# Contrast adjustment of 48 images: three bands on a 192 KB ring in pieces, instead of six tiles in three slots

## The chip, the cores and the metric

The kernel runs on one core of one Trainium2 chip; the seven other cores do nothing. The metric is the device time of one execution in microseconds. The kernel before has a median of 239.43 us over three runs (239.42 to 239.44).

## The reference

```python
# x: (16, 3, 512, 512) float32, factor = 1.5
mean = np.mean(x, axis=(2, 3), keepdims=True)
out = np.clip(mean + factor * (x - mean), 0, 1).astype(np.float32)
```

There are 48 images of 262,144 float32 pixels, 1 MB each. Each needs its own mean before its first output pixel can be computed: out = clip(1.5 x - 0.5 mean). All of x is 50.33 MB, read once, and the output is as large, written once, so 100.66 MB pass between the memory and the core's on-chip buffer. The buffer that the kernel uses for pixels is 192 KB on each of 128 partitions, 25.2 MB, half of x.

## The kernel before, in words

An image lies on 16 partitions with 64 KB (16,384 elements) on each, so a tile of 128 partitions is eight images, 8.39 MB, and x is six tiles, which are contiguous in memory. `ring` has three slots of 64 KB per partition; tile t lives in slot t mod 3 from its load to its store, and is overwritten in place.

All transfers are issued by SyncE (SP) on one DMA queue, in the order of the program: `load` (L77) and `store` (L80). The order is written by hand under `tc.manual_schedule()`: loads of tiles 0, 1, 2, then computation and stores of tiles 0, 1, 2, then loads 3, 4, 5, then computation and stores 3, 4, 5. The semaphore waits are put in from the data's dependences. An instruction that SP holds for a wait holds everything behind it in SP's program; a transfer that is issued goes behind those that were issued earlier.

For each tile `compute` does the following. The sum over a partition's row is split: VectorE reduces the first 4,352 columns (L85, into `sums`), ScalarE passes the other 12,032 through a copy in place with an accumulator (L89). TensorE multiplies each column of sums by `blockw`, a 128x128 matrix that holds (1 - factor)/262144 where two partitions belong to the same image (L100); the products accumulate in the column of `bias` in PSUM that belongs to the tile. Then VectorE computes factor * x + bias (L103) and max 0, min 1 (L106), both in place, and the store is issued. Tile 0 alone is cut: it is loaded in pieces of 8, 24 and 32 KB per partition, summed in two halves, and clipped and stored in pieces of 8 and 56 KB.

Each of the 16 DMA engines moves eight of the 128 rows of a DMA, one packet a row, and then one 4-byte packet that tells the semaphore.

Of the kernel before, what the change touches and what calls it, by code (L numbers as in the profile page):

```python
# [1 line left out]

# [4 lines left out]


P = 128  # L10
ROW = 16384
HALF = ROW // 2
BUFS = 3
SHORT = 2048
SUM = 4352


@with_exitstack
def kernel(
    ctx: ExitStack,  # L20
    tc: tile.TileContext,
    x: bass.AP,
    factor: float,
    out: bass.AP,
):

    nc = tc.nc
    f32 = mybir.dt.float32  # L30
    Alu = mybir.AluOpType
    Act = mybir.ActivationFunctionType

    B, C, H, W = x.shape
    n_img, n_pix = B * C, H * W
    ppi = n_pix // ROW
    per_tile = P // ppi
    n_tiles = n_img // per_tile
    assert ppi * ROW == n_pix and per_tile * n_tiles == n_img

    factor = float(factor)
    wconst = (1.0 - factor) / float(n_pix)

    x_f = x.rearrange("b c h w -> (b c h w)")
    out_f = out.rearrange("b c h w -> (b c h w)")

    def dram(ap, t, c0=0, c1=ROW):
        return bass.AP(tensor=ap.tensor, offset=t * P * ROW + c0, ap=[[ROW, P], [1, c1 - c0]])

    consts = ctx.enter_context(tc.tile_pool(name="consts", bufs=1))  # L50
    xpool = ctx.enter_context(tc.tile_pool(name="xpool", bufs=1))
    small = ctx.enter_context(tc.tile_pool(name="small", bufs=1))
    psum = ctx.enter_context(tc.tile_pool(name="psum", bufs=1, space=bass.MemoryType.PSUM))


    sums = small.tile([P, 4 * n_tiles], f32, name="sums")
    bias = psum.tile([P, n_tiles], f32, name="bias")

    blockw = consts.tile([P, P], f32, name="blockw")
    blocks = blockw.rearrange("p (a b) -> p a b", b=ppi)  # L60
    nc.gpsimd.memset(blockw, wconst)  # L61
    for base, step in ((0, -ppi), (ppi - 1, ppi)):
        nc.gpsimd.affine_select(  # L63
            out=blocks,
            in_=blocks,
            compare_op=Alu.is_ge,
            fill=0.0,
            base=base,
            pattern=[[step, per_tile], [0, ppi]],
            channel_multiplier=1 if step < 0 else -1,  # L70
        )


    ring = xpool.tile([P, BUFS, ROW], f32, name="ring")

    def load(t, c0=0, c1=ROW):
        nc.sync.dma_start(out=ring[:, t % BUFS, c0:c1], in_=dram(x_f, t, c0, c1))  # L77

    def store(t, c0=0, c1=ROW):
        nc.sync.dma_start(out=dram(out_f, t, c0, c1), in_=ring[:, t % BUFS, c0:c1])  # L80

    def add(t, col, c0, c1, c2):
        xt = ring[:, t % BUFS, :]
        own = sums[:, 4 * t + col : 4 * t + col + 2]
        nc.vector.tensor_reduce(  # L85
            out=own[:, 0:1], in_=xt[:, c0:c1], axis=mybir.AxisListType.X, op=Alu.add
        )
        part = xt[:, c1:c2]
        nc.scalar.activation(out=part, in_=part, func=Act.Copy, accum_out=own[:, 1:2])  # L89
        return [own[:, 1:2], own[:, 0:1]]  # L90

    def compute(t, *cuts):
        xt = ring[:, t % BUFS, :]
        if t == 0:
            parts = add(t, 0, 0, SUM, HALF) + add(t, 2, HALF, HALF + SUM, ROW)
        else:
            parts = add(t, 0, 0, SUM, ROW)
        shift = bias[:, t : t + 1]
        for k, part in enumerate(parts):
            nc.tensor.matmul(shift, blockw, part, start=k == 0, stop=k == len(parts) - 1)  # L100
        for c0, c1 in zip((0, *cuts), (*cuts, ROW)):
            part = xt[:, c0:c1]
            nc.vector.tensor_scalar(  # L103
                out=part, in0=part, scalar1=factor, scalar2=shift, op0=Alu.mult, op1=Alu.add
            )
            nc.vector.tensor_scalar(  # L106
                out=part, in0=part, scalar1=0.0, scalar2=1.0, op0=Alu.max, op1=Alu.min
            )
            store(t, c0, c1)

    with tc.manual_schedule():
        load(0, 0, SHORT)
        load(0, SHORT, HALF)
        load(0, HALF, ROW)
        load(1)
        load(2)
        compute(0, SHORT)
        compute(1)
        compute(2)
        load(3)  # L120
        load(4)
        load(5)
        compute(3)
        compute(4)
        compute(5)


# [1 line left out]
_INS = ['x', 'factor']  # L129
_OUTS = [((16, 3, 512, 512), 'float32')]  # L130

_NUMBERS = {'factor': 1.5}


# [26 lines left out]
```

## Time and profile before

| | |
|---|---|
| median of three runs | 239.43 us |
| span of the profiled execution, first to last instruction | 237.30 us |
| median less span | 2.13 us |
| first DMA packet of x starts | 1.82 us |
| last packets of the last store end | 235.43 to 236.08 us |
| VectorE busy | 137.4 us (58%) |
| ScalarE busy | 59.9 us (25%) |
| TensorE busy | 7.9 us (3%) |
| DMA | 2160 packets, 100.66 MB, 98.7% of 16 engines' span |

The profiled execution is given by its span alone; the 2.13 us between the span and the median lie outside the first and last instruction. Times in the views are in microseconds from the start of the span. A GB/s figure of a stretch counts each packet where it starts.

### The profile page before, as it was taken

The page shows a single profiled execution, that of the slowest core. Times are in us where ns is not written, and L with a number is a line of the kernel's source. Part 1 is how long each engine was busy: PE and PEld are TensorE (multiplying, and loading weights), DVE is VectorE, ACT ScalarE, POOL GpSimd, SP SyncE. Part 2 cuts the span into 40 slices and gives each one's busy share as a digit, 9 for nine tenths or more (in the row PEclk, how much of TensorE's full clock was granted, in tenths as well). Part 3 has the DMA queues.
Part 4 walks back from the last instruction along what each step waited for, and adds up shares of the span by engine and source line. Part 5 has one row for each costly group of instructions (what it writes and reads, how often), then busy time and mean ns, then how long its engine had stood idle before and what let it go on. Part 6 is the DMA issues. An engine that isn't in the chain of part 4 may idle for free.

```text
span 237.3 us, 186 instructions
## 1 busy us (share of the span) xinstructions
PE 7.9 (3%) x28; PEld 6.9 (3%) x28; DVE 137.4 (58%) x21; ACT 59.9 (25%) x15; POOL 1.1 (0%) x7
## 2 busy tenths in 40 slices
PE   0010100010001000000000000100000000000000
PEld 0010100010001000000000000100000000000000
DVE  0071899949998998000000043499989998991000
ACT  2051300980492000000000049319509800000000
POOL 1000000000000000000000000000000000000000
DMA  7999989899799798989899998989899998989894
GB/s 289 418 442 442 530 353 530 353 486 398 331 464 454 341 530 353 530 353 519 365 442 442 398 486 353 530 354 530 353 475 409 431 453 376 508 353 530 353 530 177
DMA packets 2160, 100.66 MB, mean 424 GB/s; under 512 B 240, under 2 KB 240, under 8 KB 240
## 3 DMA queue, kind: packets, MB, share of 16 engines
q1 hardware_dynamic: 2160, 100.66, 98.7%
HBM read 50.33 MB, written 50.33 MB: 424 GB/s over the span
## 4 chain that ended last, share of the span: by engine, by line
DVE 43%; DMA 36%; ACT 9%; PE 2%; SPq 1%; issue 0%; DVEq 0%; ACTq 0%
DMA ring<-in_x_dram 36%; DVE ring L103 18%; DVE ring L106 18%; ACT ring L89 9%; DVE sums L85 6%; PE bias L100 2%; SPq L77 1%; SPq L80 0%; DVEq L103 0%; ACTq L89 0%
## 5 line engine op out<-in xcount | busy, mean ns | idle before, releaser
L89 ACT ACTIVATE ring<-ring 128x12032 f32<-128x12032 f32 (+1 forms) x7 | 58.0, 8280 | 128.2 <-DMA ring<-in_x_dram 128.2
L85 DVE TENSOR_REDUCE sums<-ring 128x1 f32<-128x4352 f32 x7 | 32.8, 4683 | 63.9 <-DMA ring<-in_x_dram 63.9
L103 DVE TENSOR_SCALAR ring<-ring,bias 128x16384 f32<-128x16384 f32 (+2 forms) x7 | 52.8, 7538 | 12.9 <-PE bias L100 12.9
L106 DVE TENSOR_SCALAR ring<-ring 128x16384 f32<-128x16384 f32 (+2 forms) x7 | 52.3, 7476 | 0.2
L100 PE MATMUL bias<-sums,blockw 128*128 128x1 f32 x28 | 7.9, 360 | 189.1 <-ACT ring L89 175.4
L100 PEld LDWEIGHTS bias<-sums,blockw 128*128 128x128 f32 x28 | 6.9, 314 | 190.0 <-ACT ring L89 159.4
L89 ACT ACT_TABLE_LOAD x1 | 1.3, 1283 | 0.8 <-PEq L142 0.8
L89 ACT ACTIVATION_READ_ACCUMULATOR ring<-ring 128x1 f32 x7 | 1.3, 187 | 0.0
L63 POOL TENSOR_SCALAR_AFFINE_SELECT blockw<-blockw 128x128 f32<-128x128 f32 x2 | 0.7, 340 | 0.1
L61 POOL MEMSET blockw<- 128x128 f32 x1 | 0.2, 204 | 0.3 <-POOLq L142 0.3
L142 POOL MEMSET const-bfloat16-1.0<- 128x1 bf16 x1 | 0.1, 102 | 0.0
L142 POOL MEMSET const-uint8-127<- 128x1 uint8 x1 | 0.1, 102 | 0.0
L142 POOL MEMSET const-float32-0.0<- 128x1 f32 x1 | 0.1, 98 | 0.3 <-issue 0.3
L142 POOL MEMSET const-float32-1.0<- 128x1 f32 x1 | 0.1, 98 | 0.0
## 6 DMA issues: line engine op xcount, KB each, us to landing
out_dram<-ring SPq DMA_DIRECT2D x1, 7168.0 KB, 35.9
ring<-in_x_dram SPq DMA_DIRECT2D x1, 4096.0 KB, 20.8
ring<-in_x_dram SPq DMA_DIRECT2D x1, 3072.0 KB, 11.6
ring<-in_x_dram SPq DMA_DIRECT2D x1, 1024.0 KB, 4.7
out_dram<-ring SPq DMA_DIRECT2D x1, 1024.0 KB, 34.3
ring<-in_x_dram SPq DMA_DIRECT2D x5, 57.7
out_dram<-ring SPq DMA_DIRECT2D x5, 27.0
```

What stands on the lines that cost most here:

```text
L61: nc.gpsimd.memset(blockw, wconst)
L63: nc.gpsimd.affine_select(out=blocks, in_=blocks, compare_op=Alu.is_ge, fill=0.0, base=base, pattern=[[step, per_tile], [0, ppi]], channel ...
L77: nc.sync.dma_start(out=ring[:, t % BUFS, c0:c1], in_=dram(x_f, t, c0, c1))
L85: nc.vector.tensor_reduce(out=own[:, 0:1], in_=xt[:, c0:c1], axis=mybir.AxisListType.X, op=Alu.add)
L89: nc.scalar.activation(out=part, in_=part, func=Act.Copy, accum_out=own[:, 1:2])
L100: nc.tensor.matmul(shift, blockw, part, start=k == 0, stop=k == len(parts) - 1)
L103: nc.vector.tensor_scalar(out=part, in0=part, scalar1=factor, scalar2=shift, op0=Alu.mult, op1=Alu.add)
L106: nc.vector.tensor_scalar(out=part, in0=part, scalar1=0.0, scalar2=1.0, op0=Alu.max, op1=Alu.min)
L142: nc = _bacc.Bacc("TRN2", target_bir_lowering=False, num_devices=1)
```

## The change

An image now lies on eight partitions with 128 KB (32,768 elements) on each, so 128 partitions hold a band of sixteen images, and x is three bands of 16.8 MB. The ring is the same 192 KB per partition, now without slots: the column c (0 to 384 KB over the three bands) lives at c mod 192 KB. Loads, sums, clips and stores are written in column pieces, named here in KB per partition; band 0 is 0 to 128, band 1 is 128 to 256, band 2 is 256 to 384. The 15 DMAs become 24: 12 loads and 12 stores, of 8, 24, 32 or 64 KB per partition. In memory the rows of a DMA are now 128 KB apart, before 64 KB. A shared piece is summed by VectorE (44%) and ScalarE (56%), a piece with `shared=False` by ScalarE alone. All transfers stay on SP's one queue.

```diff
-ROW = 16384
-HALF = ROW // 2
-BUFS = 3
-SHORT = 2048
-SUM = 4352
+ROW = 32768
+KB = 256
+RING = 192 * KB
+SHARE = 0.56
...
-    ring = xpool.tile([P, BUFS, ROW], f32, name="ring")
+    ring = xpool.tile([P, RING], f32, name="ring")
+    def piece(c0, c1):
+        first = c0 % RING
...
+        return ring[:, first : first + c1 - c0]
-    def load(t, c0=0, c1=ROW):
-        nc.sync.dma_start(out=ring[:, t % BUFS, c0:c1], in_=dram(x_f, t, c0, c1))
+    def load(*edges):
+        for c0, c1 in zip(edges, edges[1:]):
+            nc.sync.dma_start(out=piece(c0 * KB, c1 * KB), in_=dram(x_f, c0 * KB, c1 * KB))
...
+    def add(*edges, shared=True):
+        for c0, c1 in zip(edges, edges[1:]):
+            band = c0 * KB // ROW
+            shift = bias[:, band : band + 1]
+            begin, end = c0 * KB == band * ROW, c1 * KB == (band + 1) * ROW
+            mid = c0 * KB + (round((c1 - c0) * KB * (1 - SHARE) / 64) * 64 if shared else 0)
+            parts = []
+            if shared:
...
+                nc.vector.tensor_reduce(
+                    out=own, in_=piece(c0 * KB, mid), axis=mybir.AxisListType.X, op=Alu.add
+                )
...
+            part = piece(mid, c1 * KB)
+            nc.scalar.activation(out=part, in_=part, func=Act.Copy, accum_out=own)
...
+                nc.tensor.matmul(
+                    shift, blockw, own, start=begin and k == 0, stop=end and k == len(parts) - 1
+                )
+    def clip(*edges):
...      # per piece: the two tensor_scalar as before, then store(c0, c1)
     with tc.manual_schedule():
-        load(0, 0, SHORT)
-        load(0, SHORT, HALF)
-        load(0, HALF, ROW)
-        load(1)
-        load(2)
-        compute(0, SHORT)
-        compute(1)
-        compute(2)
-        load(3)
-        load(4)
-        load(5)
-        compute(3)
-        compute(4)
-        compute(5)
+        load(0, 8, 32, 64, 96, 128, 160, 192)
+        add(0, 8, shared=False)
+        add(8, 32, 64, 96, 128)
+        add(128, 160, 192, shared=False)
+        clip(0, 8, 32, 64, 96, 128)
+        load(192, 224, 256, 320)
+        add(192, 224, 256)
+        clip(128, 160, 192)
+        add(256, 320, shared=False)
+        load(320, 352, 384)
+        clip(192, 256)
+        add(320, 352, 384)
+        clip(256, 288, 320, 352, 384)
```

More of the change, by code (lines that the diff above doesn't have):

```diff
@@ L36 @@
     ppi = n_pix // ROW
-    per_tile = P // ppi
-    n_tiles = n_img // per_tile
-    assert ppi * ROW == n_pix and per_tile * n_tiles == n_img
+    per_band = P // ppi
+    n_bands = n_img // per_band
+    assert ppi * ROW == n_pix and per_band * n_bands == n_img
     factor = float(factor)
@@ L45, with dram @@
     out_f = out.rearrange("b c h w -> (b c h w)")
-    def dram(ap, t, c0=0, c1=ROW):
-        return bass.AP(tensor=ap.tensor, offset=t * P * ROW + c0, ap=[[ROW, P], [1, c1 - c0]])
+    def dram(ap, c0, c1):
+        band, col = divmod(c0, ROW)
+        return bass.AP(
+            tensor=ap.tensor, offset=band * P * ROW + col, ap=[[ROW, P], [1, c1 - c0]]
+        )
     consts = ctx.enter_context(tc.tile_pool(name="consts", bufs=1))
@@ L53 @@
     psum = ctx.enter_context(tc.tile_pool(name="psum", bufs=1, space=bass.MemoryType.PSUM))
-    sums = small.tile([P, 4 * n_tiles], f32, name="sums")
-    bias = psum.tile([P, n_tiles], f32, name="bias")
+    sums = small.tile([P, 32], f32, name="sums")
+    bias = psum.tile([P, n_bands], f32, name="bias")
     blockw = consts.tile([P, P], f32, name="blockw")
@@ L68 @@
             base=base,
-            pattern=[[step, per_tile], [0, ppi]],
+            pattern=[[step, per_band], [0, ppi]],
             channel_multiplier=1 if step < 0 else -1,
         )
-    ring = xpool.tile([P, BUFS, ROW], f32, name="ring")
-    def load(t, c0=0, c1=ROW):
-        nc.sync.dma_start(out=ring[:, t % BUFS, c0:c1], in_=dram(x_f, t, c0, c1))
[L79 to L104, printed above, removed]
+    ring = xpool.tile([P, RING], f32, name="ring")
@@ new lines, in piece, with store @@
+    def piece(c0, c1):
+        first = c0 % RING
+        assert c0 // ROW == (c1 - 1) // ROW and first + c1 - c0 <= RING
+        return ring[:, first : first + c1 - c0]
+    def load(*edges):
+        for c0, c1 in zip(edges, edges[1:]):
+            nc.sync.dma_start(out=piece(c0 * KB, c1 * KB), in_=dram(x_f, c0 * KB, c1 * KB))
+    def store(c0, c1):
+        nc.sync.dma_start(out=dram(out_f, c0 * KB, c1 * KB), in_=piece(c0 * KB, c1 * KB))
+    used = [0]
+    def add(*edges, shared=True):
[6 more added lines that the diff above has]
+            if shared:
+                own = sums[:, used[0] : used[0] + 1]
+                used[0] += 1
+                nc.vector.tensor_reduce(
+                    out=own, in_=piece(c0 * KB, mid), axis=mybir.AxisListType.X, op=Alu.add
+                )
+                parts.append(own)
+            own = sums[:, used[0] : used[0] + 1]
+            used[0] += 1
+            part = piece(mid, c1 * KB)
+            nc.scalar.activation(out=part, in_=part, func=Act.Copy, accum_out=own)
+            parts.append(own)
+            for k, own in enumerate(parts):
+                nc.tensor.matmul(
+                    shift, blockw, own, start=begin and k == 0, stop=end and k == len(parts) - 1
+                )
@@ L105, in compute @@
+    def clip(*edges):
+        for c0, c1 in zip(edges, edges[1:]):
+            band = c0 * KB // ROW
+            part = piece(c0 * KB, c1 * KB)
+            nc.vector.tensor_scalar(
+                out=part,
+                in0=part,
+                scalar1=factor,
+                scalar2=bias[:, band : band + 1],
+                op0=Alu.mult,
+                op1=Alu.add,
             )
@@ L108, in compute @@
             )
-            store(t, c0, c1)
+            store(c0, c1)
     with tc.manual_schedule():
-        load(0, 0, SHORT)
-        load(0, SHORT, HALF)
-        load(0, HALF, ROW)
-        load(1)
-        load(2)
-        compute(0, SHORT)
-        compute(1)
-        compute(2)
-        load(3)
-        load(4)
-        load(5)
-        compute(3)
-        compute(4)
-        compute(5)
+        load(0, 8, 32, 64, 96, 128, 160, 192)
[11 more added lines that the diff above has]
+        clip(256, 288, 320, 352, 384)
 _INS = ['x', 'factor']
```

## The prediction

> **What bounds the kernel now.** I read the page first, its DMA rows and its queue.
>
> ```profile
> span 237.3 us, 186 instructions
> ...
> PE 7.9 (3%) x28; PEld 6.9 (3%) x28; DVE 137.4 (58%) x21; ACT 59.9 (25%) x15; POOL 1.1 (0%) x7
> ...
> DMA  7999989899799798989899998989899998989894
> ...
> q1 hardware_dynamic: 2160, 100.66, 98.7%
> ...
> DVE 43%; DMA 36%; ACT 9%; PE 2%; SPq 1%; issue 0%; DVEq 0%; ACTq 0%
> ```
>
> The chain gives VectorE 43% and the DMA 36%, yet the one queue's engines are occupied for 98.7% of the span. The packet records decide: put end to end, each engine's 135 packets run from 1.82 us to between 235.43 and 236.08 us without a gap (each starts 3 or 4 ns before its predecessor ends). So no wait of the chain reaches the end time: the queue always had the next transfer. The end is the sum of the packets, plus 1.82 us in front and 1.22 us from the last packet to the end of the span.
>
> Packets have fixed durations by row: 8 KB 0.309 us, 24 KB 0.912, 32 KB 1.213, 56 KB 2.116, 64 KB 2.418, in both directions. The exceptions are in the next view, the windows (length, engines' busy times, granted clock, DMA share, GB/s).
>
> ```profile
> 38.60:57.92 19.32, 1.01 (x4) 0.93 (x4) 16.25 (x3) 10.32 (x2) 0.00 (x0) 1.00 1.00 434
> 57.92:61.36 3.44, 0.00 (x0) 0.00 (x0) 3.44 (x1) 0.00 (x0) 0.00 (x0) 1.00 1.03 305
> ...
> 155.55:174.90 19.35, 1.17 (x4) 1.00 (x4) 18.56 (x4) 10.32 (x2) 0.00 (x0) 1.00 1.00 434
> 174.90:177.46 2.56, 0.00 (x0) 0.00 (x0) 2.56 (x1) 0.00 (x0) 0.00 (x0) 1.00 0.99 410
> ```
>
> Each first window holds eight 64 KB rows per engine, the second the last row of load 2 and of load 5. After each the queue turns from loads to stores. There all sixteen rows took longer than 2.418 us: 3.532 on average at the first turn, 2.55 at the second. A turn from loads to stores cost 1.11 and 0.13 us. The turn back (load 3 after store 2, near 122 us) lengthened one row of one engine by 0.19, a mean of 0.01. Beyond the start-up no other row is long.
>
> **The change, part by part.** The head is the same: the first loads are again 8, 24 and 32 KB. So is the tail from last packet to end.
>
> Row pieces. With the 4 ns overlap a 64 KB row costs 2.4145 us of an engine, two 32 KB rows 2 x 1.2095 = 2.419: a split costs 4.5 ns. Per engine there were 15 DMAs x 8 = 120 rows, now 24 x 8 = 192: 72 x 4.5 ns = 0.32 us. Nine more semaphore packets of 9 ns less overlap: 0.05. Together +0.37 us. A Trainium skill rule speaks against this edit: "DMA: Bandwidth & Descriptors", Anatomy of one DMA, gives each (GpSimd-issued) DMA about 2.0 us of fixed cost; nine more in series would be 18 us, some 257 us in all. The trace disagrees for queued transfers: across its 14 boundaries the next packet follows within nanoseconds.
>
> Turns. Loads turn to stores at load 160-192, load 256-320 and load 352-384: three times, not twice. The first again leads from loads into an 8 KB store, the first store of all, as the 1.11 did; I carry it over. Of the other two one replaces load 5 (0.13). The new one lies between 0.13 and 1.11; by its row sizes (64 KB load, 32 KB store) it is nearest to 0.13, where a 64 KB store followed; for its smaller rows I take 0.30. Nothing excludes that 32 KB rows make turns cheaper; that is a rival. The second turn back is 0.01.
>
> Engines and waits cost nothing if the queue stays fed, so I walked the queue. Prices come from the groups by shape.
>
> ```profile
> L89 ACT ACTIVATE ring<-ring 128x12032 f32<-128x12032 f32 x5 | 51.2, 10231 | 111.2 <-DMA ring<-in_x_dram 111.2
> L103 DVE TENSOR_SCALAR ring<-ring,bias 128x16384 f32<-128x16384 f32 x5 | 43.8, 8757 | 12.3 <-PE bias L100 12.3
> L106 DVE TENSOR_SCALAR ring<-ring 128x16384 f32<-128x16384 f32 x5 | 43.5, 8695 | 0.2
> L85 DVE TENSOR_REDUCE sums<-ring 128x1 f32<-128x4352 f32 x7 | 32.8, 4683 | 63.9 <-DMA ring<-in_x_dram 63.9
> ...
> L89 ACT ACTIVATE ring<-ring 128x3840 f32<-128x3840 f32 x2 | 6.8, 3402 | 17.0 <-DMA ring<-in_x_dram 17.0
> L103 DVE TENSOR_SCALAR ring<-ring,bias 128x2048 f32<-128x2048 f32 x1 | 1.3, 1292 | 0.7 <-PE bias L100 0.7
> L106 DVE TENSOR_SCALAR ring<-ring 128x2048 f32<-128x2048 f32 x1 | 1.2, 1227 | 0.0
> ```
>
> Two shapes of a row give a slope: ScalarE (10.231 - 3.402)/8192 = 0.83 ns a column plus 0.2 us, each clip pass 0.521 plus 0.2. A 32 KB piece (8,192 columns) then takes 2 passes, 4.48 + 4.43 = 8.9 us on VectorE, against 8 x 1.2095 = 9.68 us on the queue: VectorE gains 0.8 us on it with every piece. Its share of a sum (3,584 columns) takes 3.9 us by L85's mean, ScalarE's 4,608 columns 4.0 plus 0.2 to read the accumulator; landing follows the last packet by 0.3, the matmuls take 0.6.
>
> The walk, with 19.3 us for a 64 KB piece on the queue:
> - Load 96-128 lands at 41.6 us; sums and matmul end at 46.6; clips of band 0 end at 49, 56, 65, 74 and 83. The queue is busy with loads to 61.8 (where it was before too), then runs out after each store at 64, 72, 81, 91, 101. Each store is issued over 5 us ahead.
> - SP then holds load 192-224 (wait on stores 0-8 and 8-32, long landed) and 224-256, issued about 84; load 256-320 waits for store 96-128, 101 us, with 19 us of loads queued. Behind it on SP stand stores 128-160 and 160-192, not computed yet.
> - Load 224-256 lands at about 120.3. VectorE has its reduces first, ScalarE ends at 124.6, matmul 125.2, clip 128-160 ends at 134.2, and SP issues at 134.6. The queue has load 256-320 until 139.2. With 0.6 us from issue to packet, 4 us are to spare. This is the tightest place.
> - Load 320-352 waits for store 128-160 (about 149.7) while 160-192 still has 9 us to run; load 352-384 likewise. Store 192-256, behind both on SP, is issued at 161 with the queue full to 178. The 64 KB ScalarE sum 256-320 (13.9 us from 139.5) is done at 153.4; nobody needs it before 178.
> - Load 352-384 lands at 178.6, clip 256-288 ends at 192.5, the queue is busy with store 192-256 to 198: 4.5 us to spare. The last three stores gain 0.8 us each.
>
> So nothing runs dry. Before, store 5 was issued at 214.6 with store 4's last packets landing at 217.1, a margin of 2.5 us less the 0.6, and lost nothing.
>
> The sum: +0.37 + 0.30 + 0.01 = +0.68. The profiled span of 237.30 becomes 237.98; the median stands 2.13 us above it, so 240.11, said as 240.1. The nearest row alone (0.13) gives 239.94, the far end (1.11) 240.92.
>
> **Rivals.**
> - No change that shows (chance 0.16): 32 KB rows make the new turn free, or two turns cheaper; 239.43 + 0.37 = 239.8. A measurement of this kernel can tell about 0.2%, 0.48 us, from no change, which would hide this. For it: the second turn was only 0.13.
> - Faster (0.10): the excess of a turn belongs to the row size. The long rows were 64 KB; now two of three turns end on 32 KB loads, the first included. If the three together cost 0.2 us instead of the 1.24 of before, it is 0.37 - 1.04 = -0.67: 238.8. It decides once the three sum to under 0.39. Against it: both turns of before ended on 64 KB rows and differ eightfold, so the load's row size is not what sets it.
> - The queue runs dry (0.06): store 128-160 is issued too late because band 1's sums end later than I count. It decides from 4 us; every microsecond beyond is lost for good, since the end is the sum of packets and gaps. Sums 6 us late would cost 2: 242.1. For it: VectorE and ScalarE both work on the last piece at once, which L85 and L89 did before too. Against: their instructions repeat to some 10 ns in the trace.
> - The row pitch (0.08): the 128 streams lie 128 KB apart instead of 64. One per cent on 232 us of packets is 2.3 us, so 242.4 with the sum; it decides from 0.2%, a 32 KB row of 1.216 us. Against: rows of 8, 24, 32 and 56 KB on the 64 KB pitch fit one line with the contiguous ones. The Trainium skill ("DMA: Bandwidth & Descriptors", Latency and other measured facts) reports HBM copies slowing with large power-of-two pitches, 207 GB/s at 512 KiB where a padded pitch gave 214, and more beyond; it has no figure for 128, and no run here shows one.
>
> **How the numbers follow.** The forecast has 0.60 as slower by over 0.2%; with pitch and dry queue that is 0.74. Same 0.16, faster 0.10. The range goes from 239.4 (free turns and somewhat less) to 241.6 (the far end of the turn, plus a dry spell or pitch loss of 0.7 us), leaving out most of the faster case and the worse halves of the last two.
>
> **What would show it.** 3,456 packets; 32 KB rows at 1.213 us; the queue at 434 GB/s between turns; long rows only ahead of stores 0-8, 128-160 and 192-256; store 128-160 issued near 134.6; span near 238.0. A gap in the engines' packets near 139 or 198, or 32 KB rows above 1.216 us, makes it wrong on the slow side; a total of turns under 0.39 us on the fast side.

## The result, and the profile after

The changed kernel takes 258.51 us (median of four runs, 258.17 to 259.07) against 239.43 in the same comparison: a ratio of 1.0795, 95% interval 1.0779 to 1.0811. It is 19.1 us slower, where 0.7 us slower was forecast. The profiled execution took 258.63 us and its span is 256.9, 1.7 less. Later executions of the kernel before show the same 1.7 (239.44 us with a span of 237.7), so the profiled execution of before was probably some 0.4 us faster than its median, and only 1.7 of the 2.13 us lie outside the span. That would account for the spans differing by 19.6 us and the medians by 19.1.

The page after, the lines that answer to those shown of before:

```profile
span 256.9 us, 233 instructions
...
PE 10.4 (4%) x40; PEld 9.4 (4%) x40; DVE 136.3 (53%) x32; ACT 63.6 (25%) x25; POOL 1.2 (0%) x7
...
DMA  7999999993037899998999999999999998999996
...
q1 hardware_dynamic: 3456, 100.66, 91.9%
...
DMA 45%; DVE 38%; ACT 6%; SPq 2%; PE 1%; another core or an unknown queue 1%; issue 0%
```

The packet count is the 3,456 that was forecast, and VectorE's busy time hardly differs from before. But the queue's share fell from 98.7% to 91.9%, and the row of slices shows where: "9303" is a hole near 60 to 85 us, and nothing like it follows. The windows of the changed kernel put edges on the hole (columns as before; the last two are DMA share and GB/s):

```profile
0.00:61.00 61.00, 5.20 (x20) 4.72 (x20) 14.61 (x4) 25.99 (x13) 1.22 (x7) 1.00 0.97 413
61.00:72.90 11.90, 0.59 (x2) 0.50 (x2) 3.38 (x3) 7.12 (x2) 0.00 (x0) 1.00 0.00 0
72.90:75.50 2.60, 0.00 (x0) 0.00 (x0) 2.57 (x2) 0.00 (x0) 0.00 (x0) 1.00 0.98 403
75.50:79.80 4.30, 0.00 (x0) 0.00 (x0) 4.30 (x2) 0.00 (x0) 0.00 (x0) 1.00 0.17 74
79.80:87.10 7.30, 0.00 (x0) 0.00 (x0) 7.26 (x2) 0.00 (x0) 0.00 (x0) 1.00 0.91 387
87.10:88.60 1.50, 0.00 (x0) 0.00 (x0) 1.50 (x2) 0.00 (x0) 0.00 (x0) 1.00 0.51 218
88.60:255.76 167.16, 4.64 (x18) 4.21 (x18) 102.73 (x22) 30.49 (x10) 0.00 (x0) 1.00 0.99 425
```

The loads end at 61 us and for 11.9 us nothing moves; then stores 0-8, 8-32 and 32-64 run with smaller holes in front of the second and third. In the packet records the three holes have a mean of 17.84 us per engine. After 88.6 us the queue is fed to the end. What the first store waited for stands in the timeline of the changed kernel (start, length, instruction, and in brackets the idle time before it with its releaser):

```profile
46.22 1.01 PE L111 MATMUL bias<-sums,blockw 128*128 128x1 f32 x4 [8.69 <-DVE sums L101]
...
51.99 7.03 ACT L108 ACTIVATE ring<-ring 128x8192 f32<-128x8192 f32 x1 [5.58 <-DMA ring<-in_x_dram]
...
61.69 7.03 ACT L108 ACTIVATE ring<-ring 128x8192 f32<-128x8192 f32 x1 [2.58 <-DMA ring<-in_x_dram]
...
68.86 0.59 PE L111 MATMUL bias<-sums,blockw 128*128 128x1 f32 x2 [9.11 <-ACT ring L108]
69.49 1.29 DVE L119 TENSOR_SCALAR ring<-ring,bias 128x2048 f32<-128x2048 f32 x1 [23.33 <-PE bias L111]
...
72.07 0.35 SPq L86 DMA_DIRECT2D out_dram<-ring  x1
```

Band 0's last matmuls are over at 47.2 us. The first clip of band 0 starts at 69.49, directly behind the matmuls of pieces 128-160 and 160-192, which belong to band 1. It reads another column of `bias`, and needs nothing of them. In the built program its wait is for the eleventh matmul of the program; band 0 has nine (each is two instructions in the timeline).

### The profile page after: what moved, and what is told of

The parts are those of the page before. It is cut to its first block, busy times and chain, and to the rows that moved or that the text cites. A ratio compares the mean times of both kernels' runs of the same rounds, so it can differ in the third digit from the quotient of the medians.

```text
span 256.9 us, 233 instructions
## 1 busy us (share of the span) xinstructions
PE 10.4 (4%) x40; PEld 9.4 (4%) x40; DVE 136.3 (53%) x32; ACT 63.6 (25%) x25; POOL 1.2 (0%) x7
## 2 busy tenths in 40 slices
DMA packets 3456, 100.66 MB, mean 392 GB/s; under 512 B 384, under 2 KB 384, under 8 KB 384
## 3 DMA queue, kind: packets, MB, share of 16 engines
q1 hardware_dynamic: 3456, 100.66, 91.9%
## 4 chain that ended last, share of the span: by engine, by line
DMA 45%; DVE 38%; ACT 6%; SPq 2%; PE 1%; another core or an unknown queue 1%; issue 0%
DMA ring<-in_x_dram 39%; DVE ring L119 17%; DVE ring L127 17%; DMA out_dram<-ring 7%; ACT ring L108 6%; DVE sums L101 3%; SPq L83 1%; PE bias L111 1%; SPq L86 0%
## 5 line engine op out<-in xcount | busy, mean ns | idle before, releaser
L108 ACT ACTIVATE ring<-ring 128x4608 f32<-128x4608 f32 (+4 forms) x12 | 61.2, 5101 | 137.8 <-DMA ring<-in_x_dram 137.8
L119 DVE TENSOR_SCALAR ring<-ring,bias 128x8192 f32<-128x8192 f32 (+3 forms) x12 | 53.8, 4487 | 37.7 <-PE bias L111 37.7
L101 DVE TENSOR_REDUCE sums<-ring 128x1 f32<-128x3584 f32 (+1 forms) x8 | 30.1, 3768 | 64.1 <-DMA ring<-in_x_dram 64.1
L127 DVE TENSOR_SCALAR ring<-ring 128x8192 f32<-128x8192 f32 (+3 forms) x12 | 53.1, 4427 | 0.4
L111 PE MATMUL bias<-sums,blockw 128*128 128x1 f32 x40 | 10.4, 358 | 192.6 <-DVE sums L101 134.2
L111 PEld LDWEIGHTS bias<-sums,blockw 128*128 128x128 f32 x40 | 9.4, 320 | 193.5 <-DVE sums L101 134.8
L108 ACT ACTIVATION_READ_ACCUMULATOR ring<-ring 128x1 f32 x12 | 2.2, 186 | 0.0
## 6 DMA issues: line engine op xcount, KB each, us to landing
ring<-in_x_dram SPq DMA_DIRECT2D x1, 3072.0 KB, 11.9
```

The source lines that it names most:

```text
L101: nc.vector.tensor_reduce(out=own, in_=piece(c0 * KB, mid), axis=mybir.AxisListType.X, op=Alu.add)
L111: nc.tensor.matmul(shift, blockw, own, start=begin and k == 0, stop=end and k == len(parts) - 1)
L119: nc.vector.tensor_scalar(out=part, in0=part, scalar1=factor, scalar2=bias[:, band : band + 1], op0=Alu.mult, op1=Alu.add,)
L127: nc.vector.tensor_scalar(out=part, in0=part, scalar1=0.0, scalar2=1.0, op0=Alu.max, op1=Alu.min)
```

## The experiments

Theory A: the first clip waits for matmuls of band 1 that are written ahead of it and write the same PSUM tile, and this empties the queue. Rival B: each of the nine more DMAs costs some 2 us, which would give nearly the same total. Rival C: the rows 128 KB apart are slower.

**One bias tile for each band.**

```diff
-    bias = psum.tile([P, n_bands], f32, name="bias")
+    bias = [psum.tile([P, 1], f32, name=f"bias{k}") for k in range(n_bands)]
...  # bias[:, band : band + 1] becomes bias[band][:, 0:1] in add and in clip
```

> The changed kernel with one edit: bias is three PSUM tiles of one column, one for each band, instead of one tile of three columns, so that the first clip no longer waits for the sums of pieces 128-160 and 160-192. Theory A (the first clip's wait on band 1's matmuls emptied the queue): the clip of piece 0-8 starts near 47 us instead of 69.5, the three gaps in the DMA engines' packets (11.9 + 4.3 + 1.4 us on the first engine) vanish, and the time is 240.1 to 241.5 us. Rival B (each of the nine more DMAs costs about 2 us): 258.5 us, unchanged. Rival C (rows 128 KB apart are slower): at most 1 or 2 us below 258.5.

Measured: 239.56 us (median of 11), 1.0006 times the kernel before, interval 0.9995 to 1.0017. Its timeline and the windows over the place of the hole:

```profile
46.14 1.01 PE L111 MATMUL bias<-sums,blockw 128*128 128x1 f32 x4 [8.70 <-DVE sums L101]
47.19 1.29 DVE L119 TENSOR_SCALAR ring<-ring,bias 128x2048 f32<-128x2048 f32 x1 [1.10 <-PE bias L111]
...
51.91 7.03 ACT L108 ACTIVATE ring<-ring 128x8192 f32<-128x8192 f32 x1 [5.58 <-DMA ring<-in_x_dram]
53.11 3.36 DVE L127 TENSOR_SCALAR ring<-ring 128x6144 f32<-128x6144 f32 x1
...
134.53 9.21 SPq L86 DMA_DIRECT2D out_dram<-ring  x2
```

```profile
61.00:72.90 11.90, 0.59 (x2) 0.50 (x2) 11.87 (x3) 7.12 (x2) 0.00 (x0) 1.00 1.02 438
72.90:88.60 15.70, 0.00 (x0) 0.00 (x0) 10.13 (x3) 0.00 (x0) 0.00 (x0) 1.00 1.00 434
```

The clip's idle time fell from 23.33 to 1.10 us and the holes are gone, with all 24 DMAs and the 128 KB spacing kept. This one wait made the whole loss that can be seen in the time; B and C are out. That it came out 0.5 us under the lower end expected is taken up below.

**The same adds, written later.**

```diff
-        add(128, 160, 192, shared=False)
         clip(0, 8, 32, 64, 96, 128)
+        add(128, 160, 192, shared=False)
```

> The changed kernel with one line moved: add(128, 160, 192, shared=False) behind clip(0, 8, 32, 64, 96, 128), with the single bias tile kept. Theory A: the same cure as separate bias tiles, since what the clip waits for is what was written down before it: 240.1 to 241.5 us, within 0.3 us of the kernel with three bias tiles. Rival A2 (it is VectorE and TensorE using one PSUM bank that costs, not the order written down): stays near 258. Rivals B and C: near 258.5.

Measured: 239.53 us (median of 11), ratio 1.0006, interval 0.9997 to 1.0014. Rival A2 is out: with a single `bias` tile kept, the order written down decides. (TensorE and VectorE take turns at the tile here, as the waits below show; what their using it at once would do is not shown.) The false dependences that remain, in the waits of this kernel (who waited for whom, total, times, longest):

```profile
PE bias L111 <- DVE ring L119: 31.6, 1, 31.6
DVE ring L119 <- PE bias L111: 14.6, 4, 11.2
```

Now the matmuls of band 1 wait 31.6 us for the clips of band 0 that read the tile, and clip 192-256 waits 11.2 us for the sum of piece 256-320 in band 2. Neither costs anything: nobody needs those matmuls before 125 us, and store 192-256, issued at 172.4, still finds the queue busy until 178.

**A late first clip planted in the kernel before.** No DMA changes; only the sums and matmuls of later tiles are written ahead of tile 0's clip.

```diff
-        compute(0, SHORT)
-        compute(1)
-        compute(2)
+        total(0)       # sums and matmuls of one tile
+        total(1)
+        total(2)       # in the smaller dose this stands behind clip(1)
+        clip(0, SHORT) # the two passes and the stores
+        clip(1)
+        clip(2)
```

> The kernel before with the same fault planted: the sums and matmuls of tile 1 are written ahead of the clip of tile 0, all else and every DMA as before. Theory A: clip 0 starts at 53.4 instead of 27.9 us, store 0's second piece is issued at 71.7 with the queue empty from 64.3; gaps of 8.0, 0.5 and 3.4 us: about 251 us. Rivals B and C: no DMA has changed, 239.4 us.

> The kernel before with a larger dose: the sums and matmuls of tiles 1 and 2 both ahead of the clip of tile 0. Theory A: clip 0 starts at 74 us, gaps of about 15.5 us before the first store and 12.7 before the second: about 267 us (266.7 if the long rows at the first turn also go, since no store is queued behind the loads). Rivals B and C: 239.4 us.

Measured: 252.77 us for the smaller dose, 268.80 for the larger (medians of two runs each), both 1.8 us above the forecast. The first clip and the windows of the larger dose:

```profile
61.33 4.69 DVE L85 TENSOR_REDUCE sums<-ring 128x1 f32<-128x4352 f32 x1 [14.66 <-DMA ring<-in_x_dram]
...
72.75 1.29 DVE L106 TENSOR_SCALAR ring<-ring,bias 128x2048 f32<-128x2048 f32 x1 [6.74 <-PE bias L99]
```

```profile
0.00:60.70 60.70, 3.33 (x12) 2.93 (x12) 14.06 (x3) 18.60 (x7) 1.09 (x7) 1.00 0.97 415
60.70:76.20 15.50, 1.01 (x4) 0.93 (x4) 8.10 (x4) 10.32 (x2) 0.00 (x0) 1.00 0.01 3
76.20:78.70 2.50, 0.00 (x0) 0.00 (x0) 2.50 (x1) 0.00 (x0) 0.00 (x0) 1.00 0.97 403
78.70:91.50 12.80, 0.00 (x0) 0.00 (x0) 12.77 (x3) 0.00 (x0) 0.00 (x0) 1.00 0.05 22
```

Holes of 15.5 and 12.8 us were forecast as 15.5 and 12.7. Per engine the packet records have 11.7 us of holes in the smaller dose and 28.8 in the larger: 239.44 plus these is 251.2 and 268.3. The rest, 1.6 and 0.5 us, is near what longer rows add in the records (1.8 and 0.9). So a late first store makes this kind of loss on contiguous tiles and with 15 DMAs. The cause of the lateness is not the same alone: tile 0's clip stands here behind VectorE's own reduces of later tiles too. In the larger dose the last reduce ends at 66.0, and only the 6.74 us from there to 72.75 are the wait for matmuls; in the smaller dose it is again 6.74 us, from 46.7 to 53.39. The two doses show what an empty queue costs; that the wait on `bias` empties it in the changed kernel rests on the experiments before and on the next one, where VectorE has nothing else ahead of the clip.

**Half of the wait.** One of band 1's two sums stays ahead of the clips.

```diff
-        add(128, 160, 192, shared=False)
+        add(128, 160, shared=False)
         clip(0, 8, 32, 64, 96, 128)
+        add(160, 192, shared=False)
```

> The changed kernel, single bias tile, with only half of the wait: add(128, 160) stays ahead of the clips of band 0, add(160, 192) goes behind them. The first clip then waits for the matmuls of 128-160 alone (ScalarE done at 59.1 in the changed kernel). Theory A: clip 0-8 starts near 59.8 us; walked through the queue, gaps of 2.0, 4.7 and 1.5 us before stores 0-8, 8-32 and 32-64, so 8.2 us above the 239.56 of the kernel with separate bias tiles, less 0.6 us of its long rows at the first turn: 247.1 us. If a wait costs all its length and not what is left after the queue's stock (rival A3), 12.6 us of delay of the first clip against 47.2 us cost 12.6: 252.2 us.

Measured: 248.38 us (median of two runs), against 247.1 forecast.

```profile
59.47 1.29 DVE L119 TENSOR_SCALAR ring<-ring,bias 128x2048 f32<-128x2048 f32 x1 [13.62 <-PE bias L111]
```

The first clip started at 59.47, 12.3 us later than with separate tiles, and the holes were 2.3, 4.2 and 1.5 us, 8.0 per engine. The forecast had 8.2. It missed because it took 0.6 us off for shorter rows, and in the records the rows are 1.1 us longer in sum than with separate tiles. A delay of the first clip costs only what is left of it when the queue's stock of loads is used up, and then again at the next stores until VectorE has caught up: the second and third hole are 4.2 and 1.5 us here and in the changed kernel alike, whatever the length of the wait. Rival A3 is out.

**Every DMA in 8 KB pieces**, on the kernel with separate bias tiles.

```diff
-        for c0, c1 in zip(edges, edges[1:]):
+        for c0 in range(edges[0], edges[-1], 8):
+            c1 = c0 + 8
             nc.sync.dma_start(out=piece(c0 * KB, c1 * KB), in_=dram(x_f, c0 * KB, c1 * KB))
...  # the stores likewise
```

> The kernel with separate bias tiles, every DMA cut into 8 KB pieces: 96 DMAs instead of 24, the same sums, clips and order. Prediction's price of a split (rows of 8 KB cost an engine 0.3055 us, so 768 x 0.3055 = 234.6 against 232.2, and 72 semaphore packets of 5.5 ns): +2.8 us, 242.4 us, packets without a gap. Rival B in its weakest form, 2 us for each of 72 more DMAs even when they are queued: over 380 us.

Measured: 243.17 us (median of four), 1.0153 times the kernel before (1.0140 to 1.0167), and 3.6 us above the one with 24 DMAs: 0.05 us for each of 72 more.

```profile
DMA  7999999999999999999999999999999999999995
...
DMA packets 13825, 100.68 MB, mean 417 GB/s; under 512 B 1536, under 2 KB 1536, under 8 KB 1536
...
q1 hardware_dynamic: 13824, 100.67, 99.4%
```

The queue's share of the span is higher than in any other kernel here, and yet the time is 3.6 us longer than with 24 DMAs: with the queue fed, it is the packets' own sum that counts. The forecast of 242.4 was 0.8 us low; 8 KB rows took 0.311 us on average instead of 0.309, which is 768 x 0.002 = 1.5 us, and the long rows at the turns (0.8 us with 24 DMAs) all but vanished.

**Tile 0 whole**, on the kernel before.

```diff
-        load(0, 0, SHORT)
-        load(0, SHORT, HALF)
-        load(0, HALF, ROW)
+        load(0)
...
-        compute(0, SHORT)
+        compute(0)
```

> The kernel before with tile 0 loaded whole and stored whole: 12 DMAs of 64 KB per partition, no 8, 24, 32 or 56 KB pieces. If the long rows of the first turn (1.11 us) belong to the 8 KB store behind them, as the prediction took them, they fall to about 0.1 and the time to 238.3 us. If they are a property of any turn with stores already queued, whose size varies by chance, the time is 239.3 (the 24 fewer rows give 0.1 us) and cannot be told from the kernel before. Queue fed throughout: tile 0 lands at 21.5, its store is issued near 50, before the loads end at 62.

Measured: 239.43 us (median of 11), ratio 0.9998, interval 0.9986 to 1.0009: the same. Its first turn, in windows:

```profile
38.60:57.90 19.30, 1.18 (x4) 1.00 (x4) 18.51 (x4) 10.32 (x2) 0.00 (x0) 1.00 1.01 435
57.90:61.36 3.46, 0.00 (x0) 0.00 (x0) 3.46 (x1) 0.00 (x0) 0.00 (x0) 1.00 1.02 303
```

The last row of load 2 is as long as before (303 GB/s against 305) with a 64 KB store behind it. The 8 KB store was not the cause. No kernel of this study beats the one before.

## Why the prediction was wrong

The bound was read rightly: the end is the sum of packets and gaps on one queue. The step that failed is the first item of the walk, "Load 96-128 lands at 41.6 us; sums and matmul end at 46.6; clips of band 0 end at 49, 56, 65, 74 and 83." The sums did end there (matmuls over at 47.2). But the clip was taken to wait for its own band's matmuls alone. `add(128, 160, 192, shared=False)` stands ahead of `clip(0, ...)` and writes the same `bias` tile, so the clip's wait covered it too, and ended at 69.5. The walk followed what the data need. The program waits for what was written down before, and for `bias` it does so by the whole tile: a reader of one column waits for the matmuls into the others. This does not hold for every tile. In `ring` the columns are kept apart: with separate bias tiles ScalarE passes piece 128-160 from 51.91 to 58.94 us while VectorE clips piece 8-32 of the same `ring` from 53.11 on. Whether the unit for `bias` is the tile or the PSUM bank (a section of PSUM) in which it lies, no run here separates: in the built program the three separate tiles lie in three banks. In the kernel before, each clip directly follows its own matmuls, so its trace could not show the difference, and the rest of the walk inherited the mistake.

- The rival with the dry queue (0.06) had the right mechanism at the wrong place: it looked at store 128-160, the tightest margin, and not at the first store, where I counted over 5 us to spare. The price was 17.8 us of holes, not 2.
- The rest of the walk held once the wait was gone. With separate bias tiles the first clip started at 47.19 and store 128-160 was issued at 134.53, against 134.6.
- Row pieces, +0.37 us: 32 KB rows stayed at 1.213 us. The ratio of 1.0006 with its interval is -0.12 to +0.41 us, which holds the 0.37 and does not by itself show it; the 8 KB kernel does show a small price per piece.
- Turns, +0.31: not borne out. With separate tiles the three turns to stores cost 0.64, 0.10 and 0.06, in sum 0.80 against the 1.24 of before, where the forecast carried 1.54. That is in line with 240.1 being 0.5 us above the 239.56 measured without the wait. But these are single profiled executions, and with the adds written later the same turns cost 1.1 at the same median, so the size of a turn is not settled. (At the second turn of before, fifteen of the sixteen rows were long, not all.)
- Row pitch: nothing. The queue moved 434 to 438 GB/s in the windows of 128 KB rows shown above. The Trainium skill's slowdown for large power-of-two pitches ("DMA: Bandwidth & Descriptors", Latency and other measured facts), which it gives for 512 KiB and more, is not seen at 128 KB.
- Rival B came near the measured 19 us by luck. The holes stand in three places only, the repaired kernel keeps all 24 DMAs at 239.56, and 72 more cost 0.05 us each. The Trainium skill's fixed cost of about 2.0 us per DMA (same page, Anatomy of one DMA), which it gives for DMAs issued from GpSimd, would make an estimate of 18 us for nine more in series. On SP's queue, with a next transfer waiting, the traces show no such cost.

Of the 19.41 us by which the engines' last packets end later (255.19 against 235.78 on average), holes are 17.84, longer rows 1.1 (at turns, in the start-up, and by some nanoseconds each behind the holes) and row pieces 0.37 by the prediction's price, which leaves 0.1.

## What to carry to other kernels

When a change moves one tile's producers ahead of another tile's consumer, look at what the consumer's wait counts, not only at what it needs: columns of the PSUM tile `bias` that different steps write were one thing to the waits here, while pieces of `ring` were not. Give such results a tile each, or write the later producer behind the earlier consumer; either cured this kernel. And on a kernel that one queue bounds, check the margin of the first store after a long run of loads first, because the stock of queued loads is what pays for every wait ahead of it.

## What was not expected of the hardware

The last row of a transfer before the queue turns was longer by over 0.1 us only where the next transfer was already queued, and by amounts that the row size alone does not explain. The first turn to stores cost 1.11 us in the kernel before and 0.64 and 1.02 in the two repaired kernels, nearly nothing with 8 KB rows, and nothing where the queue was empty. Later turns differ between kernels: load 256-320, of 64 KB rows, cost 1.05 us in the changed kernel and 0.10 with separate tiles; the turn from stores to loads 0.79 and nothing. Each figure is from one profiled execution. What sets it is open; it accounts for a microsecond or two here.
